# A router that reads the residual rows, and a top-k that is sorted tile by tile

## The chip, the cores and the metric

The kernel runs on one core of a Trainium2 chip. Times are microseconds on the device for one execution; the profile is of one such execution. TensorE is PE in the profile (PEld its weight loads), VectorE is DVE, ScalarE is ACT, GpSimd is POOL, and SP only issues DMAs.

## The reference, cut to what matters

One layer of a diffusion backbone with 1024 latent tokens of width 1024: attention (two head groups), an output projection, a gated residual, and a mixture of 16 experts in which each expert picks its own 128 tokens. What the change touches is the way from the projection to the choice of tokens:

```python
x = x + g_a * mix                                        # mix: output projection
h2 = modulate(rmsnorm(x, norm_ffn[l]), sh_f, sc_f)       # h * (1 + scale) + shift
x = x + g_f * ec_moe(h2, w_router[l], w_gate[l], w_up[l], w_down[l])
...
aff = jax.nn.softmax(jnp.einsum('bnd,de->bne', h, w_router), axis=-1)
vals, idx = lax.top_k(jnp.swapaxes(aff, 1, 2), cap)      # cap = 128, for each of 16 experts
```

The kernel needs, for each expert, the 128th largest affinity (`thr1`): a token is taken where its affinity reaches that threshold.

## The kernel before, in words

The program is written in one order for each engine; nothing is scheduled on its own, and each engine works through its instructions in that order and waits where an operand is not there. Behind the attention stands the output projection over eight tiles of 128 tokens. Tile `t` is eight steps `omm(t, k, k + 1)` of six matmuls each (two halves of 512 columns, three products of split numbers). The last tile does its two halves one after the other. The mix of tile 0 arrives in parts; its step 7 needs a slice that comes by DMA last (`mix7`, split by `msplit7`). Right behind that split VectorE finishes `scf`, the row of norm weight times (1 + scale), repeated on all partitions; `shf` is the row of shifts.

Around the steps stand, for the tiles before:

- `oev(t)`: output of the projection times the gate, plus the residual (`xres`), its square on ScalarE, the RMS scale on GpSimd, and the residual written to DRAM (`accd`).
- `oev2(t)`: `h2`, the normed and modulated rows, from `xres`, the scale, `scf` and `shf`; two operations for each half. For the first and last tile all four are on VectorE.
- `otr(t, b)`: four transposes of `h2` on TensorE and a copy on ScalarE into `th`.
- `rout(t, ...)`: eight matmuls with the router's weights `wrf`; each is two instructions in the profile.
- `soft(t)`: softmax over 16 experts, in three operations of VectorE around an exponential of ScalarE. The affinities go to `affp` (in the memory of `gfb`) and, behind the rows of `h2`, to DRAM (`h2d`), from where the experts gather their tokens.

Inside the projection `rout` and `soft` are two tiles behind. Tiles 6 and 7 have theirs behind the loop. The top-k works in three groups of tiles (0 to 3, 4 and 5, 6 and 7): `aft` transposes their affinities on TensorE so that an expert's values lie along a row, in 32 rows for each tile; `topk` sorts each half row of 64 by eight rounds of `max` (the 8 largest) and `match_replace` (which removes them), and merges sorted lists by steps of a maximum and a minimum (`stage_`). `tk_run(n)` puts the next `n` steps of that list into VectorE's order. The last group's steps stand behind all else, with what is left of the group before between them.

Behind the loop SP issues the loads of weights for which memory has come free (`w_load`); ScalarE rounds the first weights (`w_hi`), and `w_lo(0, pool)` lets GpSimd subtract them, one operation of 128 x 2048. Behind the threshold come the token numbers, the first gathers, and the experts.

Of the kernel before, what the change touches and what calls it, by code (L numbers as in the profile page):

```python
# [10 lines left out]
F32 = mybir.dt.float32  # L11
# [36 lines left out]
def tile_backbone(ctx: ExitStack, tc, x, c, ctxt, c_ctx, w_mod, b_mod, norm_attn, norm_ffn, w_in,  # L48
# [1114 lines left out]
    srt = [po.tile([128, 128], F32, f"srt{i}") for i in range(5)]  # L1163
    sry = [po.tile([64, 128], F32, f"sry{i}") for i in range(5)]
    top = [po.tile([32, 128], F32, f"top{i}") for i in range(2)]
    pool.memset(srt[2], 0.0)
    pool.memset(sry[2], 0.0)
# [57 lines left out]
    dve.scalar_tensor_tensor(scf, scf, 1.0, nfb, op0=OP.add, op1=OP.mult)  # L1225

# [20 lines left out]
    def oev2(t):  # L1247
        last = t in (0, NT - 1)
        xt = MX[t // 2][1][t % 2]
        h2 = OE[t][1]  # L1250
        r = OR.pop(t)
# [8 lines left out]
    def otr(t, b):  # L1260
# [9 lines left out]
    TOP = {}  # L1270

    def topk(bufs, n, prev, dst, en):
        w, ls, za, zb = bufs[0], bufs[1], bufs[-2], bufs[-1]
        sh = bufs[2]
        p = 32 * n
        out = []

        def rnd(r, c):
            v = w[:p, 64 * c:64 * c + 64]
            o = ls[:p, 64 * c + 8 * r:64 * c + 8 * r + 8]  # L1280
            dve.max(out=o, in_=v)

        def rem(r, c):
            v = w[:p, 64 * c:64 * c + 64]
            o = ls[:p, 64 * c + 8 * r:64 * c + 8 * r + 8]
            dve.match_replace(out=v, in_to_replace=o, in_values=v, imm_value=-1.0)

        def half(p, s, o):
            x, y = s[:p, 0:64], s[:p, 64:128][:, ::-1]
            en.tensor_max(o[:p, 0:64], x, y)  # L1290
            en.tensor_tensor(out=o[:p, 64:128], in0=x, in1=y, op=OP.min)

        def stage_(s, o, p, d):
            v = lambda x: x[:p].rearrange("p (b c d) -> p b c d", c=2, d=d)
            i, o = v(s), v(o)
            en.tensor_max(o[:, :, 0], i[:, :, 0], i[:, :, 1])
            en.tensor_tensor(out=o[:, :, 1], in0=i[:, :, 0], in1=i[:, :, 1], op=OP.min)

        def clean(s, p, d, last):
            x, y = (za, zb) if s is not za else (zb, za)  # L1300
            while d:
                o = last if d == 1 and last is not None else x
                out.append(lambda s=s, o=o, d=d: stage_(s, o, p, d))
                s, x, y = o, y, x
                d //= 2
            return s

        for r in range(8):
            out.append(lambda r=r: (rnd(r, 0), rnd(r, 1)))
            if r < 7:  # L1310
                out.append(lambda r=r: (rem(r, 0), rem(r, 1)))
        out.append(lambda: half(p, ls, za))
        s = clean(za, p, 32, None)
        while n > 1:
            n //= 2

            def shift(s=s, n=n):
                if n == 2:
                    en.tensor_copy(sh[0:32], s[32:64])
                    en.tensor_copy(sh[64:96], s[96:128])  # L1320
                else:
                    en.tensor_copy(sh[0:32], s[p // 2:p // 2 + 32])

            q = 96 if n == 2 else 32
            out.append(shift)
            o = za if s is not za else zb
            out.append(lambda s=s, o=o, q=q: en.tensor_max(o[:q], s[:q], sh[:q, ::-1]))
            s = clean(o, q, 64, dst if n == 1 and prev is None else None)
        if prev is not None:
            o = za if s is not za else zb  # L1330
            out.append(lambda s=s, o=o: en.tensor_max(o[:32], prev[:32], s[:32, ::-1]))
            if dst is None:
                out.append(lambda o=o: dve.tensor_reduce(out=thr1, in_=o[:32], axis=AX.X, op=OP.min))
            else:
                clean(o, 32, 64, dst)
# [8 lines left out]
    def rout(t, k0, k1):  # L1344
        if k0 == 0:
            PR[t] = pso.tile([128, NE], F32, "r", bufs=1)
        for k in range(k0, k1):
            pe.matmul(PR[t], TH[t][:, k], wrf[:, k], start=(k == 0), stop=(k == 7))

    def soft(t):  # L1350
# [4 lines left out]
        dve.tensor_reduce(out=nm[:, 0:1], in_=pr, axis=AX.X, op=OP.max, negate=True)  # L1355
        act.activation(lg, pr, AF.Exp, bias=nm[:, 0:1], accum_out=nm[:, 1:2])
# [4 lines left out]

    def aft(t, n, bufs, prev, dst, en):
        pt = pso.tile([128, 128], F32, "q", bufs=1)[:32 * n]
        pe.transpose(pt, affp[:, t:t + n].rearrange("p a b -> p (a b)"), ident)
        act.activation(bufs[0][:32 * n], pt, AF.Copy)
        return topk(bufs, n, prev, dst, en)
# [49 lines left out]
    G0, G1 = dve, dve  # L1416
    TS = {5: (0, 0, 0, 0, 4, 4, 4, 4), 6: (4, 4, 4, 4, 4, 4, 0, 0), 7: (0,0,0,4,4,6,3,0)}
    X0 = 10
# [390 lines left out]
```

## Time and profile before

| what | value |
| --- | --- |
| median of three runs | 1235.39 us (1234.12 to 1238.19) |
| the profiled execution | 1235.9 us, its span 1234.0 us |
| busy in the span: PE, DVE, ACT, POOL | 91%, 73%, 57%, 41% |
| 757 to 852 us, output projection: PE busy | 94.12 of 95 us |
| 852 to 881.2 us, up to the threshold: PE, DVE busy | 8.14 and 25.43 of 29.2 us |
| 881.2 to 890.7 us, up to the first expert's rows: PE, DVE busy | 2.52 and 7.40 of 9.5 us |
| 890.7 to 1234 us, experts and end: PE busy | 319.99 of 343.3 us |

The span goes from the first to the last instruction; the execution's own time is 1.9 us longer. Busy shares over the whole span say little here: the stretches show where TensorE, the busiest engine, has nothing to do.

### The profile page before, as it was taken

Reading aid. Unit: us, or ns where it says so; the run is one execution under the profiler, and the core shown is the slowest. Engines: PE = TensorE matmul, PEld = TensorE weight load, DVE = VectorE, ACT = ScalarE, POOL = GpSimd, SP = SyncE. Lnnn points to the kernel's source line nnn. Section 1 sums busy time; section 2 is a strip of 40 time slices with the busy share of each in tenths; the row PEclk is TensorE's granted clock in tenths of the full one; section 3 lists DMA queues with packets and bytes.
Section 4 is the critical chain, followed back from the end, with each engine's and each line's share of the span. In section 5 each row is a group of like instructions: output and inputs, shape, how many; then the busy total and the mean of one; then the engine's idle time right before and its main releaser. Section 6 shows DMA issues by size and latency. Waiting matters only on the chain. (4 is left out here: it accounts for less than half of the span.)

```text
span 1234.0 us, 15216 instructions
## 1 busy us (share of the span) xinstructions
PE 1121.5 (91%) x5168; PEld 837.0 (68%) x5168; DVE 898.2 (73%) x1450; ACT 701.7 (57%) x1125; POOL 499.8 (41%) x468
## 2 busy tenths in 40 slices
PE   7799997799889889999998998997299999999993
PEld 1578786567557657766665667886277877778872
DVE  6738662565885376887878446468879999999987
ACT  5532332476876637766676673322267777677763
POOL 0464431356443235565665541452313333433214
PEclk9889999999999989999999999998599999999997
DMA  8624430001211102211110514673799999999827
GB/s 310 197 107 154 140 118 1 1 10 23 61 32 22 27 5 99 86 52 44 52 44 18 175 47 147 234 279 114 286 338 356 369 383 375 387 385 373 300 43 281
DMA packets 70193, 199.85 MB, mean 162 GB/s; under 512 B 16064, under 2 KB 24405, under 8 KB 64994
## 3 DMA queue, kind: packets, MB, share of 16 engines
q1 hardware_dynamic: 61796, 180.31, 40.6%
q0 software_dynamic: 5152, 18.52, 5.7%
q8 instruction: 40, 0.66, 0.2%
q10 hardware_dynamic: 3168, 0.06, 0.1%
q14 instruction: 37, 0.30, 0.1%
HBM read 173.91 MB, written 24.79 MB: 161 GB/s over the span
## 5 line engine op out<-in xcount | busy, mean ns | idle before, releaser
L1404 DVE TENSOR_TENSOR wl<-wst,wh 128x2048 fp32r<-128x2048 f32 x95 | 216.2, 2290 | 22.2 <-ACT wh L1398 22.2
L1398 ACT ACTIVATE wh<-wst 128x2048 fp32r<-128x2048 f32 x96 | 184.0, 1919 | 71.6 <-PE u L1575 40.9
L610 ACT ACTIVATE ph<-s 128x512 fp32r<-128x512 f32 x236 | 141.3, 599 | 86.5 <-PE s L1091 65.4
L1093 POOL TENSOR_TENSOR pl<-pf,ph 128x512 fp32r<-128x512 f32 x76 | 107.4, 1422 | 70.3 <-ACT pf L611 52.2
L611 ACT ACTIVATE pf<-s 128x512 f32<-128x512 f32 x197 | 117.1, 595 | 14.0 <-POOL pl L1093 12.5
L1093 DVE TENSOR_TENSOR pl<-pf,ph 128x512 fp32r<-128x512 f32 x84 | 82.6, 988 | 46.6 <-ACT pf L611 43.1
L981 DVE TENSOR_REDUCE mx<-m 128x1 f32<-128x512 f32 x128 | 82.6, 681 | 9.5 <-PE m L979 9.5
L1621 PE MATMUL y<-wh,shf 128*128 128x512 f32 x240 | 69.4, 400 | 0.0
L1089 PE MATMUL s<-qh,kh 97*128 97x512 f32 x160 | 65.9, 412 | 2.6 <-DMA qh<-rr 2.6
L768 POOL TENSOR_TENSOR pl<-pf,ph 128x512 fp32r<-128x512 f32 x37 | 47.6, 1287 | 47.0 <-ACT pf L611 38.4
L1104 PE MATMUL x<-pl,vh 128*65 128x512 f32 x160 | 63.3, 395 | 1.3 <-POOL pl L1093 1.3
L1090 PE MATMUL s<-ql,kh 96*128 96x512 f32 x160 | 64.0, 400 | 0.0
L1102 PE MATMUL x<-ph,vh 128*65 128x512 f32 x160 | 63.6, 397 | 0.0
L1091 PE MATMUL s<-qh,kl 96*128 96x512 f32 x160 | 63.6, 397 | 0.0
L1103 PE MATMUL x<-ph,vh 128*64 128x512 f32 x160 | 63.1, 394 | 0.0
L1543 POOL DMA_INDIRECT xg<-h2d,ix x16 | 23.6, 1474 | 91.1 <-PE t L1559 36.4
L1638 POOL DMA_INDIRECT accd<-yt,ix x7 | 34.7, 4958 | 61.2 <-DVE yt L1631 61.2
L280 PE MATMUL s<-wih,hb 128*128 128x512 f32 (+2 forms) x224 | 58.5, 384 | 0.0
L979 PE MATMUL m<-kh,qh 96*128 96x512 f32 x128 | 48.7, 423 | 7.8 <-DVE mx L981 4.2
L1638 POOL DMA_INDIRECT accd<-gab,ix x8 | 25.3, 3165 | 70.2 <-DVE gab L1631 70.2
L1621 PEld LDWEIGHTS y<-wh,shf 128*128 128x128 f32 x240 | 44.1, 189 | 9.5
L1575 PE MATMUL a<-wh,xh 128*128 128x512 f32 x120 | 50.1, 417 | 0.0
(481 smaller groups left out, 3068.5 us busy)
## 6 DMA issues: line engine op xcount, KB each, us to landing
wst<-in_w_gate_dram SPq DMA_DIRECT2D x63, 512.0 KB
wst<-in_w_up_dram SPq DMA_DIRECT2D x63, 512.0 KB
wst<-in_w_down_dram SPq DMA_DIRECT2D x31, 1024.0 KB
wm<-in_w_mod_dram SPq DMA_DIRECT2D x16, 512.0 KB
mw<-in_w_mod_dram SPq DMA_DIRECT2D x32, 256.0 KB
wst<-in_w_mod_dram SPq DMA_DIRECT2D x8, 1024.0 KB
wst<-in_w_in_dram SPq DMA_DIRECT2D x16, 360.0 KB
h2d<-h SPq DMA_DIRECT2D x8, 520.0 KB
```

The lines of the kernel that those rows point to most:

```text
L610: act.activation(ph, ps, AF.Exp, scale=scale)
L611: act.activation(pf, ps, AF.Exp, scale=scale)
L981: dve.tensor_reduce(out=st["m"][:, t, j:j + 1], in_=pm, axis=AX.X, op=OP.max)
L1089: pe.matmul(ps, kh[:, ks], qh[:, qs], start=True, stop=False)
L1090: pe.matmul(ps, kh[0:96, ks], ql[:, qs], start=False, stop=False)
L1091: pe.matmul(ps, kl[:, ks], qh[0:96, qs], start=False, stop=True)
L1093: return ph, lo, lambda: (pool if u % 2 and u < len(units) - 8 else dve).tensor_sub(lo, pf, f32(ph))
L1102: pe.matmul(xx, vv[:, kc, 0:65], ph, start=first, stop=False)
L1104: pe.matmul(xx, vv[:, kc, 0:65], lo, start=False, stop=last)
L1398: act.activation(W[i][0], staged[i], AF.Copy)
L1404: eng.tensor_sub(lo, staged.pop(i), f32(hi))
L1621: pe.matmul(py[n], a[:, k], w[b][:, n], start=(k == 0 and m == 0), stop=(k == 3 and m == 2))
```

## The change

The router's logits are computed from the residual rows themselves. Since `h2` is `xres` times the row's scale, times `scf`, plus `shf`, the logits are the scale times (`xres` times scaled weights) plus a bias. `router_cols` turns `scf` and `shf` into columns by 16 transposes of one row and multiplies the weights with them (`wrs`); `router_bias` computes the bias. Both stand in tile 0 of the projection. `otr` then transposes `xres`, `rout` uses `wrs`, and `soft` applies scale and bias; all three are now one tile behind, and those of tile 7 follow its projection at once. The transposes of affinities on TensorE go.

The top-k works on chunks of 32 tokens: `tk_sort(t)` transposes blocks of 32 x 32 on VectorE, so that 128 partitions hold 4 chunks of 32 experts' rows (16 used), and sorts 32 values by four rounds. `tk_join` and `tk_clean` merge tiles along a row: four tiles with tile 3's steps, tiles 4 to 6 with tile 6's, tile 7 and then the four chunks at the end.

```diff
+    def router_cols():
+        pt = pso.tile([128, 16], F32, "q", bufs=1)
+        for i, v in enumerate((scf, shf)):
+            for k in range(8):
+                pe.transpose(pt[:, 8 * i + k:8 * i + k + 1], v[0:1, k * 128:(k + 1) * 128], ident[0:1, 0:1])
+        act.activation(fT, pt, AF.Copy)
+        dve.tensor_mul(wrs, wrf, fT[:, 0:8, None].to_broadcast([128, 8, NE]))
+
+    def router_bias():
+        pt = pso.tile([128, NE], F32, "q", bufs=1)
+        for k in range(8):
+            pe.matmul(pt, fT[:, 8 + k:9 + k].to_broadcast([128, 128]), wrf[:, k], start=(k == 0), stop=(k == 7))
+        act.activation(rbias, pt, AF.Copy)
...
-            pe.transpose(pt[:, j * 128:(j + 1) * 128], OS[t][:, kk * 128:(kk + 1) * 128], ident)
+            pe.transpose(pt[:, j * 128:(j + 1) * 128], MX[t // 2][1][t % 2][:, kk * 128:(kk + 1) * 128], ident)
...
+    def tk_sort(t):
+        w, o = SW[:, 32 * t:32 * t + 32], SL[:, 32 * t:32 * t + 32]
+        out = [lambda: dve.transpose(w, affp[:, t])]
+
+        def rnd(r):
+            dve.max(out=o[:, 8 * r:8 * r + 8], in_=w)
+            if r < 3:
+                dve.match_replace(out=w, in_to_replace=o[:, 8 * r:8 * r + 8], in_values=w, imm_value=-1.0)
+
+        return out + [lambda r=r: rnd(r) for r in range(4)]
+
+    def tk_clean(x, y, p, n, d, last=None):
...
+        def stage_(a, b, d):
+            i, o = (v[:p, 0:n].rearrange("p (b c d) -> p b c d", c=2, d=d) for v in (a, b))
+            dve.tensor_max(o[:, :, 0], i[:, :, 0], i[:, :, 1])
+            dve.tensor_tensor(out=o[:, :, 1], in0=i[:, :, 0], in1=i[:, :, 1], op=OP.min)
...
-            pe.matmul(PR[t], TH[t][:, k], wrf[:, k], start=(k == 0), stop=(k == 7))
+            pe.matmul(PR[t], TH[t][:, k], wrs[:, k], start=(k == 0), stop=(k == 7))
...
-        dve.tensor_reduce(out=nm[:, 0:1], in_=pr, axis=AX.X, op=OP.max, negate=True)
-        act.activation(lg, pr, AF.Exp, bias=nm[:, 0:1], accum_out=nm[:, 1:2])
+        dve.scalar_tensor_tensor(lg, pr, OR.pop(t), rbias, op0=OP.mult, op1=OP.add)
+        dve.tensor_reduce(out=nm[:, 0:1], in_=lg, axis=AX.X, op=OP.max, negate=True)
+        act.activation(lg, lg, AF.Exp, bias=nm[:, 0:1], accum_out=nm[:, 1:2])
...
+            if t == 0 and k == 4:
+                router_cols()
+            if t == 0 and k == 6:
+                router_bias()
             if t >= 1 and k == 1:
                 oev2(t - 1)
...
+            if t >= 1 and k in (1, 2):
+                otr(t - 1, k - 1)
+            if t >= 1 and k == 4:
+                rout(t - 1, 0, 8)
+            if t >= 1 and k == 5:
+                soft(t - 1)
             if k == 1 and t + 1 < NT:
                 msplit(t + 1)
-            tk_run(TS.get(t, [0] * 8)[k])
+            if t >= 1:
+                tk_run(3 if k >= 6 or t == NT - 1 else 2)
+            if t == NT - 1 and k == 7:
+                otr(t, 0)
             if t == NT - 1 and k == 4:
                 oev(t, (0,))
         oev(t, (0, 1) if t < NT - 1 else (1,))
         if t == NT - 1:
-            tk_run(4)
+            otr(t, 1)
+            tk_run(6)
+            rout(t, 0, 8)
             oev2(t)
+            soft(t)
+            tk_run(99)
```

Three places in the order of the instructions. On TensorE, the last three steps of tile 0 (a step is three rows; `qb` is tile 0's mix) and the start of tile 1 (`mixh`), before:

```order
L1133 MATMUL o<-woh_7440,qb 128x512 x2
L1133 MATMUL o<-wol_7441,qb 128x512 x2
L1133 MATMUL o<-woh_7440,qb 128x512 x2
L1133 MATMUL o<-woh_7444,qb 128x512 x2
L1133 MATMUL o<-wol_7445,qb 128x512 x2
L1133 MATMUL o<-woh_7444,qb 128x512 x2
L1133 MATMUL o<-woh_7448,qb 128x512 x2
L1133 MATMUL o<-wol_7449,qb 128x512 x2
L1133 MATMUL o<-woh_7448,qb 128x512 x2
L1133 MATMUL o<-qb,mixh 128x512 x4
```

And the same three steps now, from the end of step 4 on:

```order
L1133 MATMUL o<-woh_7428,qb 128x512 x2
L1231 MATMUL q<-ident,scf 128x1 x8
L1231 MATMUL q<-ident,shf 128x1 x8
L1133 MATMUL o<-woh_7432,qb 128x512 x2
L1133 MATMUL o<-wol_7433,qb 128x512 x2
L1133 MATMUL o<-woh_7432,qb 128x512 x2
L1133 MATMUL o<-woh_7436,qb 128x512 x2
L1133 MATMUL o<-wol_7437,qb 128x512 x2
L1133 MATMUL o<-woh_7436,qb 128x512 x2
L1238 MATMUL q<-wrf,fT 128x16 x8
L1133 MATMUL o<-woh_7440,qb 128x512 x2
L1133 MATMUL o<-wol_7441,qb 128x512 x2
```

The transposes that need `scf` stand ahead of steps 5 to 7, the bias ahead of step 7.

On VectorE, what follows the last softmax (`gfb` holds its result), before:

```order
L1355 TENSOR_REDUCE nm<-r 128x1
L1357 RECIPROCAL nm<-nm 128x1
L1358 TENSOR_SCALAR gfb<-lg,nm 128x16
L1281 MAX sry_7408<-sry_7407 64x8 x2
L1286 MATCH_REPLACE sry_7407<-sry_7408,sry_7407 64x64 x2
```

And now:

```order
L1383 TENSOR_REDUCE nm<-lg 128x1
L1385 RECIPROCAL nm<-nm 128x1
L1386 TENSOR_SCALAR gfb<-lg,nm 128x16
L1302 TENSOR_TENSOR srt_7405<-srt_7404 128x8x8
L1303 TENSOR_TENSOR srt_7405<-srt_7404 128x8x8
L1302 TENSOR_TENSOR srt_7404<-srt_7405 128x16x4
L1303 TENSOR_TENSOR srt_7404<-srt_7405 128x16x4
L1302 TENSOR_TENSOR srt_7405<-srt_7404 128x32x2
L1303 TENSOR_TENSOR srt_7405<-srt_7404 128x32x2
L1302 TENSOR_TENSOR srt_7406<-srt_7405 128x64
L1303 TENSOR_TENSOR srt_7406<-srt_7405 128x64
L1332 TENSOR_TENSOR srt_7404<-top,srt_7406 128x128
```

Merges of tiles 4 to 6, of two inputs each, follow where maxima and replacements of tiles 6 and 7 followed; the sort of tile 7 comes behind seven more steps.

On SP, the end of the loop before (`h_8303` is tile 7's `h2`):

```order
L1386 DMA wst_8397<-in_w_gate_dram 128x1024
L1387 DMA wst_8397<-in_w_up_dram 128x1024
L1360 DMA h2d<-h_8218 128x1040
L1360 DMA h2d<-h_8303 128x1040
L1386 DMA wst_8478<-in_w_gate_dram 128x1024
```

And now (`h_8330` is tile 7's):

```order
L1388 DMA h2d<-h_8259 128x1040
L1259 DMA accd<-xres 128x1024
L1388 DMA h2d<-h_8330 128x1040
L1409 DMA wst_8505<-in_w_gate_dram 128x1024
L1410 DMA wst_8505<-in_w_up_dram 128x1024
```

The six loads of weights behind the loop (ten issues) stood ahead of the writes of tiles 6 and 7, and now stand behind them.

## Rows read from the trace of the kernel before

**Rows 1.** Busy time by stretch: start:end, length, busy us of each engine, clock, DMA.

```profile
core 0: us, PE busy (x) PEld busy (x) DVE busy (x) ACT busy (x) POOL busy (x), PEclk, DMA share, GB/s
852.00:881.20 29.20, 8.14 (x43) 6.97 (x42) 25.43 (x146) 9.13 (x14) 5.96 (x6) 0.57 0.81 307
...
1000.00:1050.00 50.00, 49.80 (x235) 39.98 (x234) 47.34 (x36) 35.86 (x29) 15.56 (x8) 1.00 1.02 375
```

**Rows 2.** Order of time on PE, end of the projection: start, duration, idle before.

```profile
845.39 0.30 PE L1364 MATMUL q<-ident,gfb 128*64 128x128 f32 x1 [0.88 <-DVE gfb L1358]
...
851.25 0.40 PE L1133 MATMUL o<-woh,mixl 128*128 128x512 f32 x1
...
881.15 0.28 PE L1494 MATMUL t<-ident,thr 16*128 16x16 f32 x1 [14.55 <-DVE thr L1333]
```

**Rows 3.** Order of time on DVE, the operation that finishes `scf`.

```profile
753.83 1.22 DVE L1225 SCALAR_TENSOR_TENSOR scf<-scf,h 128x1024 f32<-128x1024 f32 x1
```

**Rows 4.** Order of time on PE, steps 4 to 7 of tile 0, start of tile 1.

```profile
747.15 1.07 PE L1133 MATMUL o<-woh,qb 128*128 128x512 f32 x4
...
753.64 1.22 PE L1133 MATMUL o<-woh,qb 128*128 128x512 f32 x2 [3.15 <-ACT qb L81]
...
756.37 1.32 PE L1133 MATMUL o<-qb,mixh 128*128 128x512 f32 x4
```

**Rows 5.** Order of time on PE, router matmuls of tiles 0 and 7.

```profile
769.81 0.96 PE L1348 MATMUL r<-wrf,th 128*128 128x16 f32 x8
...
861.39 3.60 PE L1348 MATMUL r<-wrf,th 128*128 128x16 f32 x16
```

**Rows 6.** Busy time by stretch, columns as in rows 1; the clock is the third number from the end.

```profile
755.00:756.40 1.40, 1.40 (x5) 1.02 (x4) 1.40 (x4) 0.00 (x0) 0.00 (x0) 0.50 0.61 239
...
893.00:896.60 3.60, 3.60 (x10) 2.73 (x10) 2.07 (x3) 0.33 (x1) 0.17 (x1) 0.50 0.99 406
896.60:899.00 2.40, 2.40 (x11) 1.96 (x10) 0.00 (x0) 1.38 (x1) 0.01 (x1) 0.96 1.03 408
```

**Rows 7.** Order of time on DVE: one chain of merges, maxima, two chains.

```profile
862.17 0.21 DVE L1296 TENSOR_TENSOR srt<-srt 32x64 f32<-32x64 f32 x1
...
862.55 0.21 DVE L1296 TENSOR_TENSOR srt<-srt 32x64 f32<-32x64 f32 x1
...
866.95 0.35 DVE L1281 MAX8 sry<-sry 64x8 f32<-64x64 f32 x2 [0.82 <-ACT sry L1365]
...
873.66 0.21 DVE L1296 TENSOR_TENSOR srt<-srt 32x64 f32<-32x64 f32 x1
...
873.93 0.21 DVE L1296 TENSOR_TENSOR sry<-sry 64x64 f32<-64x64 f32 x1
```

**Rows 8.** Order of time on DVE, tile 7 from the residual to the softmax's end.

```profile
854.71 0.69 DVE L1239 TENSOR_TENSOR xres<-h,xres 128x512 f32<-128x512 f32 x1
...
857.44 0.75 DVE L1254 SCALAR_TENSOR_TENSOR h<-xres,rstd,scf 128x512 f32<-128x512 f32 x1 [0.60 <-POOL rstd L123]
...
860.22 0.17 DVE L1355 TENSOR_REDUCE nm<-r 128x1 f32<-128x16 f32 x1
...
865.03 0.17 DVE L1355 TENSOR_REDUCE nm<-r 128x1 f32<-128x16 f32 x1 [0.22 <-PE r L1348]
...
865.89 0.23 DVE L1358 TENSOR_SCALAR gfb<-lg,nm 128x16 f32<-128x16 f32 x1
```

**Rows 9.** Order of time on POOL, its one weight subtraction.

```profile
868.79 4.52 POOL L1404 TENSOR_TENSOR wl<-wst,wh 128x2048 fp32r<-128x2048 f32 x1 [2.35 <-DMA wst<-in_w_down_dram]
```

**Rows 10.** Order of time on DVE, two operations of one kind.

```profile
871.69 1.77 DVE L1331 TENSOR_TENSOR srt<-top,srt 32x128 f32<-32x128 f32 x1
...
880.50 0.28 DVE L1331 TENSOR_TENSOR sry<-top,sry 32x128 f32<-32x128 f32 x1
```

**Rows 11.** Costliest groups on the page: busy, mean ns, idle before.

```profile
L1398 ACT ACTIVATE wh<-wst 128x2048 fp32r<-128x2048 f32 x96 | 184.0, 1919 | 71.6 <-PE u L1575 40.9
```

**Rows 12.** Order of time on SP, the first weight load behind the loop.

```profile
855.84 0.38 SPq L1386 DMA_DIRECT2D wst<-in_w_gate_dram  x1
```

**Rows 13.** The gathered rows `xg`, all gathers: issue to landing.

```profile
DMA to landing us min/median/max: 4.5/7.8/9.0
```

More of the change, by code (lines that the diff above doesn't have):

```diff
@@ L1162, in tile_backbone @@
     po = Pool("po2", side="right")
[L1163 to L1167, printed above, removed]
+    srt = [po.tile([128, 256], F32, f"srt{i}") for i in range(5)]
+    top = po.tile([128, 128], F32, "top")
     po1 = Pool("po1")
@@ L1225, in tile_backbone @@
     dve.scalar_tensor_tensor(scf, scf, 1.0, nfb, op0=OP.add, op1=OP.mult)
+    wrs = po.tile([128, 8, NE], F32, "wrs")
+    fT = po.tile([128, 16], F32, "fT")
+    rbias = po.tile([128, NE], F32, "rbias")
+    def router_cols():
[10 more added lines that the diff above has]
+        act.activation(rbias, pt, AF.Copy)
     OE, OR = {}, {}
@@ L1250, in oev2 @@
         h2 = OE[t][1]
-        r = OR.pop(t)
+        r = OR[t]
         for n in range(2):
@@ L1265, in otr @@
             kk = 4 * b + j
-            pe.transpose(pt[:, j * 128:(j + 1) * 128], OS[t][:, kk * 128:(kk + 1) * 128], ident)
+            pe.transpose(pt[:, j * 128:(j + 1) * 128], MX[t // 2][1][t % 2][:, kk * 128:(kk + 1) * 128], ident)
         act.activation(TH[t][:, 4 * b:4 * b + 4], pt.rearrange("p (a b) -> p a b", a=4), AF.Copy)
     TK = []
[L1270 to L1275, printed above, removed]
-        out = []
[L1278 to L1335, printed above, removed]
@@ new lines, in tile_backbone @@
+    SW, SL, ZA, ZB, SH = srt
+    def tk_sort(t):
[7 more added lines that the diff above has]
+    def tk_clean(x, y, p, n, d, last=None):
+        out = []
+        def stage_(a, b, d):
+            i, o = (v[:p, 0:n].rearrange("p (b c d) -> p b c d", c=2, d=d) for v in (a, b))
+            dve.tensor_max(o[:, :, 0], i[:, :, 0], i[:, :, 1])
+            dve.tensor_tensor(out=o[:, :, 1], in0=i[:, :, 0], in1=i[:, :, 1], op=OP.min)
+        while d:
+            b = last if d == 1 and last is not None else y
+            out.append(lambda a=x, b=b, d=d: stage_(a, b, d))
+            x, y = b, x
+            d //= 2
+        return out, x
@@ L1360, in soft @@
         nc.sync.dma_start(out=h2d[t * 128:(t + 1) * 128], in_=h2)
[L1362 to L1366, printed above, removed]
+        TK.extend(tk_steps(t))
     gr = w_gate.rearrange("l e (p k) f -> (l e) p k f", k=8)
@@ L1415, in tile_backbone @@
     LD, LS, RING, NP = 12, 6, 3, 2
-    G0, G1 = dve, dve
-    TS = {5: (0, 0, 0, 0, 4, 4, 4, 4), 6: (4, 4, 4, 4, 4, 4, 0, 0), 7: (0,0,0,4,4,6,3,0)}
-    X0 = 10
     for t in range(NT):
@@ L1460, in tile_backbone @@
     LD += 2 * NX
-    rout(NT - 2, 0, 8)
-    soft(NT - 2)
-    tk_run(X0)
-    for b in range(2):
-        otr(NT - 1, b)
-    rout(NT - 1, 0, 8)
-    soft(NT - 1)
-    fl = aft(6, 2, sry, top[1], None, dve)
     for i in range(0, LS, 2):
@@ L1472, in tile_backbone @@
     w_load(LD)
-    for f in fl[:15]:
-        f()
-    for f in fl[15:-2]:
-        tk_run(1)
-        f()
-    tk_run(99)
-    for f in fl[-2:]:
-        f()
     po.close()
```

53 lines of the change are left out of this document (43 added, 10 removed).

## Prediction

> **What bounds the kernel now.** I read the stretches first, then the order of time on TensorE and on VectorE around the out-projection. TensorE is nearly always busy in the expert part (49.8 of 50 us in the sample stretch) and in the out-projection, so whatever delays the first expert matmul delays the end by as much. Between them it has almost nothing to do: 8.1 of 29.2 us in the stretch that begins as the last out-projection matmul ends [rows 1]. That matmul starts at 851.25 and runs 0.4 us; the transposed threshold `thr1` lets TensorE go on at 881.15, so the tail is 29.5 us [rows 2]. It is VectorE's: residual row, RMS scale, router, softmax, selection, one after another. Behind the threshold nothing is changed. The question is what the tail becomes, and what the work costs that is put ahead of it.
>
> **Term 1: the scaled router weights in tile 0.** `router_cols` stands on TensorE behind step 4 of tile 0 and transposes `scf`, so it waits for the operation that finishes `scf`. That one runs from 753.83 to 755.05 [rows 3]. Before, TensorE did steps 5 and 6 while the last slice of the mix tile was on its way, waited 3.15 us, and began step 7 at 753.64; tile 1 followed at 756.37 [rows 4]. Now it stops behind step 4, which ends near 747.6 (its last pair starts at 747.15), and goes on at 755.1. A wait of 3.15 us becomes one of 7.5, and steps 5 and 6, which used to lie inside the wait for the slice, come behind it. Queued behind the waiting transposes is all of TensorE's work; VectorE and ScalarE have only tile 0's evacuation to do, and wait too.
>
> What then stands before tile 1: 16 transposes, three steps, and the 16 matmul instructions of `router_bias`. A step takes 2.73 us at the half clock [rows 4], so 1.37 at the full one. Transposes of one row to a column are not in these rows; the nearest are the router's 16-column matmuls, 0.96 us for eight when the clock is up, 3.60 for sixteen when it is down [rows 5]. So 1.9 to 3.6 us for the transposes (I take 2.9, nearer to the slow end, since they follow an idle stretch) and the same bounds for the bias (I take 1.9, behind matmuls that have brought the clock back). The granted clock was 0.50, that is 1.2 GHz, after the 3.15 us wait, and at the start of the expert part, behind a long idle, it was still 0.50 at 893 to 896.6 [rows 6]. I let the first 4 us run at that level: 2.9 for the transposes and 1.1 of step 5, then 0.8 for its rest, 2.75 for steps 6 and 7 and 1.9 for the bias, so tile 1 starts at 755.1 + 9.45 = 764.5 instead of 756.4: **+8.2 us**. All at full clock it would be +6.6; with 5.9 us at the low level, as after 890.7, +9.5.
>
> **Term 2: the tiles.** Each tile of the out-projection still holds eight transposes and 16 router matmuls, only one tile later in the work. Residual rows are ready in time for transposes behind step 1: they are the very operations that had to be done for the norm. One router group more (tile 6's) now falls inside, at 1.7 us; the wait of 0.88 us on the transpose of the affinities goes [rows 2]: **+0.8 us**. The new sorting on VectorE lies in its free time there. If that cover were gone, a late `xres` would hold TensorE at the transposes behind step 1; I see about 1 us of margin, and cost it at nothing. The last matmul so moves by 9.0 us.
>
> **Term 3: the tail, counted from that matmul's end.** VectorE comes out of tile 6's sort and its first merge steps about 0.5 us late (estimate from the same rows as below). Multiply and add of the last half take 0.7 each, as the add at 854.71 did: 1.4, so 1.9. Six merge steps are queued next; a dependent step (max and min) starts 0.38 after the one before [rows 7], so 2.3, to 4.2. The RMS scale is ready 2.73 us after the add starts (854.71 to 857.44 before [rows 8]), at 3.9, so it no longer holds anything. The four operations for `h2` take 2.8 (857.44 to 860.22), to 7.0. The router matmuls are done under them, since they now need no norm. Softmax takes 1.1 (865.03 to the end of the operation at 865.89) and 0.2 for the new scale-and-bias, to 8.3; before it ended at 14.5. Then everything that is left: 12 steps of tile 6's merge, 4.6; the sort of tile 7, four rounds of one maximum and one replacement that wait for each other. Two independent maxima took 0.35 [rows 7]; I estimate 0.5 a round, 2.2 with the transpose. Then one merge, seven steps at 0.38, two copies and a maximum (0.8), seven steps, and a copy, a maximum and the reduction (0.9): 7.4. That ends at 22.5, against 29.5: **-7.0 us**, with -6 and -8 as bounds.
>
> **Term 4: GpSimd's subtraction in the chain.** `w_lo(0, pool)` takes 4.52 us [rows 9]. Before, it ran while VectorE did maxima and replacements, which kept their pace; but the first operation with two SBUF inputs behind them, the merge at 871.69, took 1.77 us and ended with GpSimd's, while its like at 880.50 took 0.28 [rows 10]. Now ScalarE reaches the first `w_hi` right behind the last exponential, at about 7.9, which at 1.9 us [rows 11] lets GpSimd start at 9.8, in the midst of the 12 merge steps, all of two inputs. VectorE then stands until 14.3: **+4.4 us**. If GpSimd gets in only when the sort begins, VectorE waits for what is left behind it, +2.6; if it never holds a merge, 0.
>
> The Trainium skill says the same of the place, in "SBUF — State Buffer", section "SBUF: two separate sides": GpSimd and a VectorE operation with two SBUF inputs take one pair of ports by an exclusive lock, held for the whole instruction, and whichever comes first keeps the other out. The 1.77 us agree. By the row alone only 1.5 us of such a stop have been seen, and with that the sum would be +3.5; by the rule all of GpSimd's 4.5 us lie in the chain, +6.5.
>
> **Sum.** 8.2 + 0.8 - 7.0 + 4.4 = +6.4 us on the profiled execution's own 1235.9 us (span 1234.0 and 1.9 around it): 1242.3. That execution is 0.5 above the median of the runs, so **1242**. A difference under 0.3% (3.7 us) can't be told from none here; slower begins at 1239.1, faster at 1231.7.
>
> **Rivals.**
> - *GpSimd doesn't block the merges.* Its operation would have to fall into the sort or behind the chain. For it: VectorE's steps follow each other with hardly a gap. Against: it needs only one gap, and the merge at 871.69 was kept out. It gives +2.0, and then the threshold comes early enough for the next rival to take 1 to 2: 1237 to 1239.
> - *The weight loads collide with the gathers.* On SP the six loads behind the last tile now stand behind the write of tile 7's `h2`, which waits for its softmax. They start near 869.5 rather than 855.84 [rows 12]. Seven loads of 1 MB and the `h2` write need about 21 us at the rate of this stretch, to 891; the first gather is due near 892. If they run longer, the gather takes nearer to 7.8 us (the median under load) than 4.5 (the least) [rows 13]: +3.3 and more, 1246.
> - *The new tail outweighs the front: faster.* If merge steps ran at the pace of independent ones (two chains took 0.27 for a pair of steps, 873.66 to 873.93, so 0.135 an operation [rows 7]), the some 67 operations behind the last softmax would need 9.0 us, not 14.2: -5.2. With no block by GpSimd: +8.2 + 0.8 - 7.0 - 5.2 = -3.2, and with the front at its lower bound -4.8: 1231 to 1233. It decides from 0.2 us a step on. The 0.38 of a single chain speaks against it.
> - *No change in the sum.* Front at its lower bound, tail at its best, half of the block: 6.6 + 0.8 - 8.0 + 2.6, about +2: it falls in with the first rival.
>
> **How the numbers follow.** Forecast 0.58 (1238.5 to 1245, nine in ten of it over 1239.1); no block 0.19; collision or a front longer than bounded 0.14; faster by the pace or by something not seen 0.09, a part of it below 0.3%. So slower 0.52 + 0.14 + 0.02 = 0.68, same 0.06 + 0.17 + 0.01 = 0.24, faster 0.08. The range 1236 to 1247 leaves out the last case and the worst of the collision.
>
> **What would show it.** Right: TensorE idle for over 7 us ahead of the `scf` transposes, tile 1 starting 8 us later; last out-projection matmul near 860.6; one merge of VectorE of over 4 us beside GpSimd's subtraction; threshold near 887.5. Wrong: the transposes of `scf` starting before 753, or merge steps 0.2 us apart, or the tail above 30 us although nothing blocks it.

## The result, and the profile after

The changed kernel takes 1243.55 us (median of 8 runs, 1239.91 to 1245.97) against 1235.16 us for the kernel before (8 runs, 1233.46 to 1241.37). The ratio on record, taken over all of these runs and not from the two medians (which differ by 8.4 us), is 1.0059, with an interval of 1.0042 to 1.0076. The kernel is slower by 7.3 us (1235.16 times 0.0059), where 6.4 us had been forecast. The profiled execution took 1245.97 us, its span is 1244.1.

First the stretches of the changed kernel, cut at the first out-projection matmul, the start of tile 1, the last out-projection matmul, the threshold on TensorE and the first expert matmul; and one stretch within tile 0.

```profile
742.09:767.56 25.47, 19.90 (x97) 16.10 (x96) 10.62 (x14) 8.94 (x13) 2.36 (x1) 0.80 0.49 158
767.56:864.77 97.21, 95.40 (x504) 80.77 (x503) 72.22 (x186) 26.96 (x70) 35.62 (x46) 1.00 0.51 185
864.77:891.48 26.71, 3.21 (x27) 2.81 (x25) 24.40 (x96) 7.71 (x9) 5.78 (x5) 0.61 0.69 261
...
757.17:764.24 7.07, 7.07 (x28) 5.95 (x29) 1.44 (x3) 0.18 (x1) 0.00 (x0) 0.50 0.43 163
```

In the kernel before, two rows of TensorE's order of time give the ends that the rows ahead did not need, and one of ScalarE's shows when the last slice of tile 0's mix arrives (it splits the slice as soon as its DMA has landed):

```profile
737.97 1.55 PE L1133 MATMUL o<-qb 128*128 128x512 f32 x6
...
892.58 0.80 PE L1575 MATMUL a<-wh,xh 128*128 128x512 f32 x1
```

```profile
753.28 0.31 ACT L81 ACTIVATE qb<-qb 128x128 fp32r<-128x128 f32 x1 [7.88 <-DMA qb<-mixd]
```

TensorE's order of time after, at the same places and at its waits:

```profile
742.09 1.55 PE L1133 MATMUL o<-qb 128*128 128x512 f32 x6
...
757.17 1.01 PE L1231 MATMUL q<-ident,scf 1*128 1x1 f32 x8 [5.29 <-DVE scf L1222]
...
764.24 2.02 PE L1238 MATMUL q<-wrf,fT 128*128 128x16 f32 x16
...
767.56 1.07 PE L1133 MATMUL o<-qb,mixh 128*128 128x512 f32 x4
...
840.40 0.66 PE L1280 MATMUL t<-ident,xres 128*128 128x128 f32 x4 [1.81 <-POOL xres L1253]
...
864.77 0.39 PE L1133 MATMUL o<-woh,mixl 128*128 128x512 f32 x1
...
891.48 0.28 PE L1505 MATMUL t<-ident,thr 16*128 16x16 f32 x1 [22.02 <-DVE thr L1360]
...
902.96 0.80 PE L1586 MATMUL a<-wh,xh 128*128 128x512 f32 x1
```

and ScalarE's split of the same slice:

```profile
755.35 0.31 ACT L81 ACTIVATE qb<-qb 128x128 fp32r<-128x128 f32 x1 [5.84 <-DMA qb<-mixd]
```

The 10.1 us between the two spans part like this. The first out-projection matmul starts 4.12 later (742.09 against 737.97), before the first changed instruction. From there to tile 1 it is 25.47 instead of 18.40 (756.37 in [rows 4]): +7.07. From tile 1 to the last matmul 97.21 instead of 94.88 ([rows 4] and [rows 2]): +2.33. From that matmul's start to the threshold 26.71 instead of 29.90 [rows 2]: -3.19. From the threshold to the first expert matmul 11.48 instead of 11.43. The experts take 0.3 less. So the changed stretch gives +6.3 us, of 6.4 forecast; the 4.1 ahead of it are followed up below.

The +7.07 depends on the point from which one counts. The first matmul and the slice do not move together: the slice arrives 15.31 us behind the first matmul in the profile of before (753.28 less 737.97), and 13.26 behind it in this one. TensorE waits for the slice in the one kernel and for `scf`, which stands behind the slice, in the other. From the slice's arrival to tile 1 it is 3.09 us before and 12.21 now: +9.1. In all fourteen profiles of this document this distance is 11.2 to 12.5 us where the transposes wait for the slice, and 2.4 to 3.1 where they do not. Counted in this way the two profiles differ by 2.1 us of an earlier or later slice, and by 8.0 us of changed stretches.

VectorE's order of time after, from the finished `scf` to the threshold, answers [rows 3], [rows 7], [rows 8] and [rows 10]:

```profile
755.90 1.22 DVE L1222 SCALAR_TENSOR_TENSOR scf<-scf,h 128x1024 f32<-128x1024 f32 x1
...
828.59 3.45 DVE L89 TENSOR_TENSOR qb<-mix,qb 128x512 fp32r<-128x512 f32 x2
...
838.33 1.27 DVE L1252 TENSOR_TENSOR h<-o,gab 128x512 f32<-128x512 f32 x2
...
873.04 0.23 DVE L1386 TENSOR_SCALAR gfb<-lg,nm 128x16 f32<-128x16 f32 x1
...
874.76 4.59 DVE L1332 TENSOR_TENSOR srt<-top,srt 128x128 f32<-128x128 f32 x1
...
882.27 0.20 DVE L1291 MAX8 srt<-srt 128x8 f32<-128x32 f32 x1
...
882.79 0.20 DVE L1291 MAX8 srt<-srt 128x8 f32<-128x32 f32 x1
...
884.05 0.19 DVE L1336 TENSOR_TENSOR top<-top,srt 128x32 f32<-128x32 f32 x1
...
884.67 0.23 DVE L1302 TENSOR_TENSOR srt<-srt 128x64 f32<-128x64 f32 x1
...
885.06 0.23 DVE L1302 TENSOR_TENSOR srt<-srt 128x64 f32<-128x64 f32 x1
...
891.15 0.28 DVE L1360 TENSOR_REDUCE thr<-srt 32x1 f32<-32x128 f32 x1
```

and GpSimd's, beside its merge, answers [rows 9]:

```profile
874.69 4.51 POOL L1427 TENSOR_TENSOR wl<-wst,wh 128x2048 fp32r<-128x2048 f32 x1 [1.09 <-ACT wh L1421]
```

The reader is to see three things. The merge at 874.76 begins 0.07 us behind GpSimd's subtraction and ends 0.15 behind its end. A dependent step takes 0.39 (884.67 to 885.06), a round of the sort 0.52 (882.27 to 882.79). And the residual of tile 5 starts at 838.33, directly behind VectorE's sort and 2.6 us after tile 5's last matmuls (tile 6 starts at 835.70), which TensorE feels at 840.40.

### The profile page after: what moved, and what is told of

The parts are those of the page before. It is cut to its first block, busy times and chain, and to the rows that moved or that the text cites. A ratio compares the mean times of both kernels' runs of the same rounds, so it can differ in the third digit from the quotient of the medians.

```text
span 1244.1 us, 15213 instructions
## 1 busy us (share of the span) xinstructions
PE 1127.3 (91%) x5197; PEld 842.5 (68%) x5197; DVE 906.9 (73%) x1394; ACT 700.2 (56%) x1124; POOL 495.8 (40%) x466
```

## The experiments

All times of a run stand against the kernel before on the same chip. Each run has its own profile; the columns of the table are distances in it, in us: tile 1 (the front), and the last matmul, from the first out-projection matmul; the threshold from the last matmul (the tail); the first expert matmul from the threshold; and their sum from the first to the last of these points. A difference of 1 to 2 us in the front is within the scatter of the slice.

| run | median, ratio (95%) | tile 1 | last | threshold | expert | sum |
| --- | --- | --- | --- | --- | --- | --- |
| kernel before | | 18.40 | 113.28 | 29.90 | 11.43 | 154.6 |
| changed, first profile | 1243.55, 1.0059 (1.0042 to 1.0076) | 25.47 | 122.68 | 26.71 | 11.48 | 160.9 |
| changed, again | 1245.23, 1.0070 (1.0044 to 1.0096) | 25.59 | 122.86 | 26.73 | 11.52 | 161.1 |
| scaled weights in tile 1 | 1239.46, 1.0021 (1.0000 to 1.0041) | 16.87 | 119.75 | 26.73 | 11.56 | 158.0 |
| subtraction on VectorE | 1239.78, 1.0013 (0.9994 to 1.0032) | 25.53 | 122.78 | 22.45 | 11.62 | 156.9 |
| merges in every tile | 1244.60, 1.0068 (1.0044 to 1.0091) | 28.30 | 127.72 | 23.18 | 14.07 | 165.0 |
| `scf` early | 1238.57, 1.0016 (1.0002 to 1.0030) | 16.81 | 116.87 | 26.71 | 11.63 | 155.2 |
| steps in the gap | 1242.87, 1.0067 (1.0049 to 1.0085) | 25.58 | 120.75 | 26.71 | 11.49 | 159.0 |
| merges in the gap | 1241.68, 1.0045 (1.0028 to 1.0062) | 26.74 | 121.92 | 22.58 | 14.15 | 158.7 |
| all three | 1229.30, 0.9949 (0.9932 to 0.9967) | 18.11 | 115.44 | 18.87 | 14.76 | 149.1 |
| all three, loads first | 1232.43, 0.9963 (0.9947 to 0.9980) | 18.47 | 115.60 | 18.88 | 17.75 | 152.2 |
| changed, loads first | 1245.25, 1.0060 (1.0038 to 1.0082) | 25.44 | 122.65 | 26.72 | 11.59 | 161.0 |
| all three, two loads late | 1226.25, 0.9911 (0.9885 to 0.9936) | 16.64 | 114.58 | 18.92 | 11.59 | 145.1 |
| all three, again | 1230.00, 0.9937 (0.9914 to 0.9959) | 16.45 | 114.63 | 18.92 | 14.95 | 148.5 |

**The changed kernel again.** Nothing is edited.

> The changed kernel once more, unchanged. In the first pair of profiles the first out-projection matmul came 4.1 us later than before (742.09 against 737.97), although nothing ahead of it was changed. If that is the scatter of the clock from one execution to the next, this profile's first out-projection matmul lies anywhere between 735 and 743, and what belongs to the change is the same again: tile 1 of the projection starts about 7.1 us later after the first matmul than before, the last matmul 9.4, the first expert matmul 6.3; the ratio is near 1.005. If the change itself moves the work ahead (by where its memory lies), the profile again shows about 742 and the ratio near 1.008.

Its first out-projection matmul starts at 740.03, and all distances behind it agree with the first profile within 0.2 us. In the thirteen profiles of the changed kernel and its variants that start lies anywhere between 735.69 and 743.32, though none of them edits what stands ahead, but for one memset of GpSimd (0.20 us) in the six with merges in every tile; the other seven lie between 736.05 and 742.09. The 4.1 us are therefore no cost that belongs to a changed instruction. Whether 1 or 2 us on the mean do (the thirteen average 739.5, the one profile of before has 737.97) stays open.

**Term 1: the scaled weights in tile 1.**

```diff
-            if t == 0 and k == 4:
+            if t == 1 and k == 0:
                 router_cols()
-            if t == 0 and k == 6:
+            if t == 1 and k == 2:
                 router_bias()
```

> The scaled weights and the bias of the router are made in tile 1 (steps 0 and 2) instead of tile 0 (steps 4 and 6), where the row of scales has long been ready. Theory (term 1, TensorE waits for that row while steps 5 and 6 stand behind the wait): the 5.3 us of idle ahead of the transposes go and steps 5 and 6 go back into the wait for the last mix slice; left are some 3 us of TensorE for transposes and bias in tile 1. Tile 1 starts about 18.5 us after the first matmul, the last matmul some 4 us earlier than in the changed kernel: -4 us, about 1239.5. Rival (the last slice of the mix bounds the front anyway, and the work costs the same wherever it stands): tile 1 starts less than 2 us earlier, no change in the time.

TensorE's order of time in that run:

```profile
756.45 0.73 PE L1133 MATMUL o<-woh,qb 128*128 128x512 f32 x2 [2.25 <-ACT qb L81]
...
758.55 1.91 PE L1133 MATMUL o<-qb,mixh 128*128 128x512 f32 x4
...
835.45 0.90 PE L1280 MATMUL t<-ident,xres 128*128 128x128 f32 x4 [1.85 <-POOL xres L1253]
```

Steps 5 and 6 are back in the wait for the slice, and tile 1 starts 8.7 us earlier than in the changed kernel. Tile 1 then lasts 17.65 instead of 13.66: 2.8 of transposes and bias, and about 1.2 of a first step at the low clock (its first four matmuls take 1.91, against 1.07). Another 1.6 us were lost behind the wait at 835.45, below. The last matmul comes 3.1 earlier, not the 4 that were expected; in the ratio it is 0.4 to 0.5%, some 5 us. The rival is out: what the change adds to the front is the wait for `scf`, not the slice.

**Term 4: the subtraction on VectorE.**

```diff
-    w_lo(0, pool)
-    w_load(LD)
...
+    w_lo(0)
+    w_load(LD0)
```

(The seventh load, `w_load(LD0)`, is now issued behind the first gathers. The third subtraction moves from ahead of the experts into step 1 of expert 0, and a one-hot row from step 2 to step 1.)

> The subtraction of the first weights is taken from GpSimd and put on VectorE behind the first gathers; nothing runs on GpSimd during the merges. Theory (term 4, GpSimd's operation keeps a merge of two inputs out): no operation of VectorE over 1 us between the last softmax and the threshold; threshold 4.3 us earlier against the last matmul, -4.3 us, about 1239.2. Rival A (VectorE was only slow there for another reason): the long merge stays, no change. Rival B (the subtraction costs VectorE 2 us or more where the experts wait for it): threshold 4.3 us earlier, but the second product of the first expert comes late, and 1 to 4 us are given back: 1239.5 to 1243.

The same merge on VectorE in that run:

```profile
872.78 0.29 DVE L1332 TENSOR_TENSOR srt<-top,srt 128x128 f32<-128x128 f32 x1
```

It takes 0.29 instead of 4.59 us. The threshold comes 4.28 us earlier behind the last matmul, nothing is given back behind it, and the ratio falls by 0.5 to 0.6%. Both rivals are out. But 0.5 to 0.6% is 6 to 7 us, more than the block: the edit has a second effect. In the changed kernel TensorE waits, within the first expert, for one-hot rows that VectorE makes (`oh`):

```profile
912.24 1.03 PE L1537 MATMUL t<-oh,tv 128*2 128x256 bf16 x8 [1.33 <-DVE oh L1530]
```

The kernel before has the same wait of 1.33. In this run it is gone, as in all later ones with the subtraction on VectorE. From the first expert matmul to the end these five profiles take 338.6 to 340.6 us, all others 340.9 to 342.2. Only the 4.3 us of the threshold are the block.

**Merges in every tile.** Tiles 1 to 6 each merge their 32 values into `top` (eight steps behind the five of the sort); tile 7's steps are as they were.

```diff
-        if t == 3:
...
+        elif t < NT - 1:
+            lt = SL[:, 32 * t:32 * t + 32]
+            out.append(lambda: dve.tensor_max(top[:, 96:128], top[:, 96:128], lt[:, ::-1]))
+            out.append(first)
+            out += tk_clean(ZA, ZB, 128, 128, 32, top)[0]
```

> Each tile's sorted chunks are merged into the running list in that tile (13 steps each) instead of four tiles with tile 3 and three with tile 6; tile 7's own work is unchanged. Theory (terms 2 and 3: a bunch of merge steps makes the residual of tile 5's neighbour late, and 12 steps are left over for the tail): TensorE's wait of 1.8 us for the residual rows goes; behind the last softmax only tile 7's sort and two merges remain, so the threshold comes 4.6 to 5.5 us earlier after the last matmul, unless GpSimd's subtraction then blocks a later merge for its whole length; together about -6 to -7 us, 1236 to 1237.5. Rival (the steps of a tile are now more than VectorE has free in that tile): TensorE waits for the residual rows in several tiles, 1 to 2 us each, and the last matmul comes 3 us or more later: no gain.

No gain: the rival held for the tiles. One of four like rows of TensorE, 0.67 to 0.90 us each:

```profile
823.19 0.66 PE L1281 MATMUL t<-ident,xres 128*128 128x128 f32 x4 [0.90 <-POOL xres L1254]
```

The tiles took 99.42 us instead of 97.27. The front was longer as well, for a reason that the edit does not touch: the out-projection started early (735.69), the slice did not (`scf` was finished 2.2 us earlier than in the repeat, while the first matmul came 4.3 earlier). And though the threshold came 3.6 us sooner, the first expert matmul came 2.6 later behind it.

**`scf` early.** The operation goes ahead of `msplit7()`, which it does not need; its transposes go behind step 6.

```diff
-    msplit7()
     dve.scalar_tensor_tensor(scf, scf, 1.0, nfb, op0=OP.add, op1=OP.mult)
+    msplit7()
...
-            if t == 0 and k == 4:
+            if t == 0 and k == 6:
                 router_cols()
-            if t == 0 and k == 6:
+            if t == 1 and k == 2:
                 router_bias()
```

> The row of scales (scf) is finished ahead of the split of the last mix slice instead of behind it, its transposes stand behind step 6 of tile 0 (instead of step 4), the bias in step 2 of tile 1. Theory (term 1 is an order of two operations on VectorE and nothing else: the scales wait for a slice that they do not need): scf is done about 12.7 us after the first out-projection matmul, when TensorE ends step 6, so the transposes lie in the wait for the slice and cost nothing; left is the bias, 1.7 us in tile 1. Tile 1 starts 17 to 18.5 us after the first matmul, the last matmul some 117.5 to 118.5 us after it, 4 to 5 us earlier than in the changed kernel and 1 us earlier than with the work in tile 1: about -5 us. Rival (the slice decides, and the transposes take its wait's place): as with the work in tile 1, no better than 119.7.

TensorE's order of time, the transposes and step 7:

```profile
753.05 0.65 PE L1231 MATMUL q<-ident,scf 1*128 1x1 f32 x8 [0.97 <-DVE scf L1221]
753.57 0.63 PE L1231 MATMUL q<-ident,shf 1*128 1x1 f32 x8
754.34 0.72 PE L1133 MATMUL o<-woh,qb 128*128 128x512 f32 x2
```

A wait of 0.97 is left, step 7 follows without one, and the last matmul comes 6.0 us earlier than in the changed kernel: 116.87, better than the 117.5 to 118.5 expected, and the rival's 119.7 is out.

**Term 2: steps in the gap.**

```diff
+            if t >= 1 and k == 0:
+                tk_run(6)
...
-            if t >= 1:
-                tk_run(3 if k >= 6 or t == NT - 1 else 2)
+            if t >= 1 and k:
+                tk_run(3 if k == 6 or t == NT - 1 and k >= 5 else 1)
```

> Only the places of the sorting steps change: six in step 0 of a tile, where VectorE otherwise stands 2.0 us for the RMS scale, one in each of the other steps (three in step 6), so that five steps instead of eight stand behind the last softmax of a tile. Theory (term 2: the late residual rows of tile 5 are the 18 steps that tile 3 brings, in a place where VectorE has no free time): TensorE's wait of 1.84 us at the transposes of tile 5's rows falls to under 0.5, the last matmul comes 1.3 to 1.8 us earlier after the first one, and the tail is as before: about -1.6 us, just at what the comparison can tell. Rival (VectorE is late there because GpSimd's addition holds its split of the next tile for 3.45 us): the wait stays above 1.5.

TensorE's row for tile 5's rows has no wait any more:

```profile
832.49 0.60 PE L1280 MATMUL t<-ident,xres 128*128 128x128 f32 x4
```

Tile 6 lasts 13.63 instead of 15.69, the last matmul comes 1.9 to 2.1 earlier, the tail is the same. The split of the mix beside GpSimd's addition still takes 3.45 us, so it was not what made TensorE wait. The whole time does not show it (1.0067 beside 1.0059 and 1.0070).

**Merges in the gap.** The edits of "merges in every tile" and "steps in the gap" together.

> The merge of every tile's chunks into the running list, as in the run of that name, with its steps put where VectorE stands still (as in the run before). Theory (that run failed because eight more steps a tile stood ahead of the residual rows): the waits of 0.7 to 0.9 us at tiles 3 to 6 go, no wait of 1.84 either, so the last matmul comes 1.5 to 2 us earlier than in the changed kernel; behind the last softmax only tile 7's sort and two merges are left, GpSimd's subtraction holds one step for about 4 us, threshold 21.5 to 22.5 us after the last matmul instead of 26.7: together -6 us, about 0.2% above the kernel before. Rival (VectorE has no time for 13 steps a tile wherever they stand): waits above 0.5 us in three tiles or more, and no more than -4 us.

No tile waits. The tail is 22.58, just above the range expected. In it GpSimd comes in during the sort; GpSimd's row and VectorE's order of time:

```profile
873.13 4.51 POOL L1426 TENSOR_TENSOR wl<-wst,wh 128x2048 fp32r<-128x2048 f32 x1 [1.15 <-ACT wh L1420]
```

```profile
873.03 0.19 DVE L1292 MAX8 srt<-srt 128x8 f32<-128x32 f32 x1
...
873.55 0.20 DVE L1292 MAX8 srt<-srt 128x8 f32<-128x32 f32 x1
873.78 3.91 DVE L1340 TENSOR_TENSOR top<-top,srt 128x32 f32<-128x32 f32 x1
```

The round from 873.03 keeps its 0.52 us beside GpSimd; the merge behind it, 0.19 us of work in the changed kernel (at 884.05), takes 3.91. The total gain is 2.5 us in the trace, not 6: the front happened to be 1.2 longer, and again the first expert matmul stands 14.15 behind the threshold. Seven weight loads lie ahead of the gathers there; the run with the subtraction on VectorE has six at the same tail (22.45), and loses nothing behind it. That the loads are the cause is argued here; the last experiment tests it.

**All three corrections together**: `scf` early, the subtraction on VectorE, merges in the gap.

> All three corrections: scales early, the subtraction off GpSimd, merges tile by tile in VectorE's gaps. Theory (the terms are independent and add): front -5, tiles -1.8, tail 18 us after the last matmul instead of 26.7 (-8.6): about -15 us against the changed kernel, some 7 us or 0.6% faster than the kernel before. Rival A (a shorter tail meets the weight loads and the gathers, which then come late): threshold 18 us after the last matmul, but the first expert matmul more than 13 us behind the threshold (11.5 in the changed kernel), and no more than -11 us. Rival B (the experts are bound by their own loads and do not start earlier for good): the first expert matmul 15 us earlier, but the end less than 11 us earlier.

Up to the threshold the terms add up, to 115.44 for the last matmul and 18.87 for the tail, and the kernel is 0.5% faster than the one before (0.6% in the repeat). Rival A holds beside the theory: 3.2 us are lost behind the threshold. Its price does not hold: the ratio is 1.1 to 1.2% under the changed kernel's, some 14 us and not 11 at most, and a part of that is the one-hot wait which the moved subtraction takes away. Rival B is out: behind the first expert matmul the kernel takes 339.9 us (340.6 in the repeat), no more than the changed kernel's 341.1 and 342.1. TensorE's wait for the gathered rows:

```profile
885.44 1.97 PE L1570 MATMUL t<-ident,xg 128*128 128x128 f32 x8 [6.58 <-DMA xg<-h2d,ix]
```

**Loads ahead of the last rows**, on the version with all three and on the changed kernel alone: the six loads before the write of tile 7's rows.

```diff
...
     for i in range(2 * NX):
         w_load(i + LD)
+    nc.sync.dma_start(out=h2d[(NT - 1) * 128:], in_=HL[0])
```

> The kernel with all three corrections, and on SP the write of tile 7's rows put behind the six weight loads instead of ahead of them (as in the kernel before). Theory (with the short tail the weight loads and the first gathers meet: the first expert matmul comes 14.8 us behind the threshold there, 11.5 in the changed kernel): the loads start some 6.5 us earlier, are through before the first gather, which lands in about 4.5 us again, and the first expert matmul comes 11.5 to 12 us behind the threshold: -3 us against the run with all three corrections, about 0.75% faster than the kernel before. Rival (the write of the rows now waits behind six loads, and the gather waits for it): the first expert matmul more than 14 us behind the threshold, no gain or a loss.

> The changed kernel with only that order of SP: the six weight loads ahead of the write of tile 7's rows. Theory (in the changed kernel itself the loads are just through when the first gather starts, so their later place costs nothing): first expert matmul 11.4 to 11.6 us behind the threshold as without it, GpSimd's subtraction and its block as before, time within 0.2% of the changed kernel, 0.6% above the kernel before. Rival (the loads do cost the changed kernel something): the first expert matmul 2 us or more earlier behind the threshold, or the time 0.2% lower and more.

The changed kernel does not mind (11.59 for 11.52): there the loads are indeed through. The corrected version gets no better (0.9963), in its profile worse, as the rival had it. VectorE's, GpSimd's and TensorE's order of time in it, and the DMA's busy share by stretch (last number but one):

```profile
875.65 0.16 DVE L1678 TENSOR_REDUCE ix<-t 128x1 int32<-128x2 f32 x1 [0.36 <-PE t L1675]
...
877.45 4.50 DVE L1431 TENSOR_TENSOR wl<-wst,wh 128x2048 fp32r<-128x2048 f32 x2
```

```profile
877.79 2.96 POOL L1560 DMA_INDIRECT xg<-h2d,ix  x1 [15.93 <-DVE ix L1678]
```

```profile
876.50:877.50 1.00, 0.50 (x8) 0.33 (x8) 0.64 (x3) 0.00 (x0) 0.00 (x0) 0.50 0.30 119
877.50:878.50 1.00, 0.00 (x0) 0.00 (x0) 1.00 (x2) 0.00 (x0) 0.71 (x1) 0.50 0.00 0
```

```profile
886.89 1.97 PE L1576 MATMUL t<-ident,xg 128*128 128x128 f32 x8 [9.56 <-DMA xg<-h2d,ix]
```

The row numbers are ready at 875.81, but the gather starts at 877.79, when the DMA engines have just run dry. It probably waited for the rows written last, although the profile names `ix`; no run tells that apart. Then it fell beside VectorE's subtraction, and its issue took 2.96 us. From the end of the issue to the transposes it was still 6.1 us, against 3.4 in the run with the subtraction on VectorE alone (issue of 1.32 at 890.23, transposes at 894.90); what took the rest is not separated.

**Two loads late.** In the version with all three, two of the six loads (2 MB) are issued behind the first gathers.

```diff
-    for i in range(2 * NX):
+    for i in range(2 * NX - 4):
         w_load(i + LD)
...
     w_load(LD0)
+    slots[:0] = [4 + NX, 5 + NX]
+    for i in range(4):
+        w_load(i + LD1)
```

> The kernel with all three corrections, and two of the six weight loads behind the loop (2 MB) issued behind the first gathers instead of ahead of them. Theory (the short tail has too little time for 6 MB of loads and the first gathers, whatever their order): TensorE's wait for the gathered rows falls from 6.6 to about 3.5 us, the first expert matmul comes 11.5 to 12 us behind the threshold instead of 14.8, and the time is some 3 us under that of all three corrections. Rival A (the gather is late for another reason, the write of tile 7's rows or GpSimd): still 14 us and more. Rival B (the two loads are then missed by the experts, who are bound by their loads): 11.5 to 12 us, but the end no earlier.

> The kernel with all three corrections once more, as the neighbour of the run with two later loads on the same chip: first expert matmul 14 to 15 us behind the threshold, ratio to the kernel before 0.993 to 0.997.

TensorE's wait in the run with the late loads:

```profile
880.88 1.97 PE L1571 MATMUL t<-ident,xg 128*128 128x128 f32 x8 [3.41 <-DMA xg<-h2d,ix]
```

3.41 us, as in the changed kernel (3.30), and 11.59 behind the threshold. The ratio is 0.9911 beside 0.9937 for its neighbour; the two intervals overlap, but the 3.4 us between 14.95 and 11.59 are in the profiles, and as much had been expected. The experts do not miss the two loads (339.9 us behind the first expert matmul). This is the fastest version: 0.9% under the kernel before.

## Why the prediction was right

The forecast (1242, slower) held, by the mechanism that it named. That the profile's +6.3 us fall on the forecast +6.4 is in part luck: counted from the slice (or from `scf`, as the prediction counts) the terms measure +9.1, +2.3, -7.5 and +4.3, together +8.2. The two ratios of the changed kernel, 1.0059 and 1.0070, are +7.3 and +8.7 us.

- **Term 1, +8.2: measured +9.1 from the slice, +7.07 from the first matmul.** TensorE stops behind step 4 and goes on with the transposes of `scf`, as forecast. The wait was 5.29 instead of 7.5, because the slice came 2.05 us earlier against the first matmul (`scf` starts 13.81 behind it, before 15.86): that is scatter, and no part of the change. The transposes took 1.8 instead of 2.9. Against that, 7.1 us ran at a granted clock of 0.50 (757.17 to 764.24), not 4, so that the work behind the wait took 10.39 instead of 9.45; this is the size that the term had wrong. That the term is mostly an order of two operations, and little work, is shown by the run with `scf` early: tile 1 starts 2.4 us behind the slice, and left are the bias and a slow first step in tile 1.
- **Term 2, +0.8: measured +2.33.** Mis-sized. The step that failed is "I see about 1 us of margin, and cost it at nothing". Of the 13 merge steps behind tile 3's sort the last eight fall, in tile 5, between the split of the next mix (3.45 us, as in the other tiles) and the softmax and sort of tile 4; all of that stands ahead of tile 5's residual, and TensorE waits 1.81 us for it. Putting the steps elsewhere took that away: from tile 1 to the last matmul it is then 95.17 us, 0.3 over the kernel before.
- **Term 3, -7.0: measured -7.5.** From the end of the last matmul (865.16) to the threshold it is 26.3; without the 4.3 of the block 22.0, forecast 22.5. The pace of 0.39 a step and 0.52 a round was as estimated.
- **Term 4, +4.4: measured +4.3.** Here the estimate went by one row in which 1.5 us had been seen, and by the whole length of the operation. By the rule of the Trainium skill on the two sides of SBUF ("SBUF — State Buffer", section "SBUF: two separate sides") the whole subtraction lies in the chain; the trace agrees, 4.59 beside 4.51, and 0.29 once it is gone.
- **The rivals.** *GpSimd doesn't block*: out. *The loads collide*: not in the changed kernel (11.48 behind the threshold, 11.43 before), but narrowly, see below. *The tail outweighs the front*: out at the measured pace.

On the collision, the 21 us that the prediction takes for 7.5 MB do not follow from the 307 GB/s of [rows 1], which would give 24. Between 877 and 896 the DMA moved 388 GB/s, and it ran dry just as the first gather was issued (896.49). Busy time by stretch in the changed kernel (DMA's share and GB/s are the last two numbers):

```profile
877.00:896.00 19.00, 2.04 (x18) 1.57 (x18) 16.02 (x68) 1.21 (x1) 2.20 (x1) 0.50 0.99 388
896.50:897.50 1.00, 0.32 (x6) 0.24 (x7) 0.89 (x2) 0.00 (x0) 1.00 (x1) 0.50 0.16 61
```

With seven loads ahead of the gathers the collision is absent at a tail of 26.7 us and there at 22.6 and 23.2 (14.1 behind the threshold); with six it is absent at 22.5 and there at 18.9 (14.8 and 15.0); with four it is absent at 18.9 too.

Of the 10.1 us between the two spans, 2.1 are scatter of the slice's arrival. The first matmul itself scatters by 7.6 us from the earliest profile to the latest, the slice between 749.8 and 757.2 us.

## What to carry to other kernels

The small work that was put on a busy engine here cost little itself; the operand that it waited for cost the most. So look at what such an operand stands behind and whether it needs it (here one operation ahead of another, with its transposes in a wait that was there anyway, was worth 6 us). Put small work of a helper engine where that engine already stands still, counted per stretch and not over the span, and keep a long operation of GpSimd out of a chain of two-input operations on VectorE. When a stall is removed, look at what it had covered: here all seven weight loads met the gathers as soon as the threshold came 4 us sooner, and changing their order did not help, while issuing fewer of them did. And when two profiles are set against each other, count from the event that the engine really waits for: the same pair gave +7.1 us from the first matmul and +9.1 from the slice.

## What was not expected of the hardware

The same wait of 1.8 us for tile 5's rows cost TensorE's clock in one execution and not in another. In the run with the weights in tile 1, the granted clock was 0.50 and then 0.72 in the 4 us behind it, and the tile lasted 1.6 us longer than in the repeat of the changed kernel, where it stayed at 1.00. So it did in the other four profiles with this wait (1.81 to 1.84 us); what made the difference is not shown. First that run, then the repeat, busy time by stretch:

```profile
836.00:838.00 2.00, 2.00 (x7) 1.61 (x6) 0.02 (x1) 2.00 (x7) 0.94 (x3) 0.50 0.61 244
838.00:840.00 2.00, 2.00 (x10) 1.62 (x9) 2.00 (x3) 0.72 (x2) 1.19 (x1) 0.72 0.05 18
```

```profile
838.50:840.50 2.00, 1.98 (x11) 1.68 (x12) 0.51 (x1) 2.00 (x6) 0.42 (x3) 1.00 0.32 127
```

GpSimd is slowed by VectorE as well: its issue of a gather took about 1.3 us alone, and longer where VectorE's subtraction ran beside it. In the fastest version the two issues stand one behind the other, and VectorE's subtractions run from 877.58 to 882.07, beside the second alone:

```profile
876.24 1.32 POOL L1555 DMA_INDIRECT xg<-h2d,ix  x1 [14.24 <-DVE ix L1673]
877.94 2.77 POOL L1555 DMA_INDIRECT xg<-h2d,ix  x1 [0.39 <-DVE ix L1673]
```

In the run with all three and the loads first, where the subtraction starts 0.34 us ahead of the first issue, it is the first that is long (2.96 us, shown above); the second, beside the subtraction's last 0.9 us, takes 1.71.
